# Attention of a hybrid decoder layer on one core: query blocks ascending in every head, K and V loaded in halves of the keys, Q tiles loaded one block further ahead

## The chip, the cores and the metric

The kernel runs on one core of a Trainium2 chip. The metric is the device time of one execution in microseconds (us). The kernel before was run three times: 1775.66, 1776.54 and 1775.54 us, median 1775.66.

## The reference

One decoder layer over 2048 tokens of width 1024. A projection of x gives latents for attention, two mixer inputs u and v, and gates; eight causal attention heads with 64 + 32 (rotary) columns of q and k and 64 of v run beside a spatial gating unit; both are gated, merged, projected and normalised.

```python
h = jnp.einsum('bsd,dn->bsn', x, w_in[l]) + b_in[l]
c_q, c_kv, k_pe, z_a, u, v, z_b, g_a, g_b = split_columns(h)
y_a = mla_attention(c_q, c_kv, k_pe, cos, sin, g_q[l], w_uq[l], g_kv[l], w_ukv[l]) * jax.nn.silu(z_a)
y_b = spatial_gating(u, v, sgu_ln_g[l], sgu_ln_b[l], w_s[l], b_s[l]) * jax.nn.silu(z_b)
merged = (jax.nn.sigmoid(g_a) * jnp.einsum('bsc,cd->bsd', y_a, w_oa[l])
          + jax.nn.sigmoid(g_b) * jnp.einsum('bsc,cd->bsd', y_b, w_ob[l]))
x = layer_norm(DN_ALPHA * x + jnp.einsum('bsd,de->bse', merged, w_out[l]), ln_g[l], ln_b[l])
# inside mla_attention, for every head and block of queries
s = jnp.einsum('bqhd,bkhd->bhqk', q[:, start:end], k[:, :end]).astype(jnp.float32) * scale
p = jax.nn.softmax(jnp.where(causal, s, -jnp.inf), axis=-1)
outs.append(jnp.einsum('bhqk,bkhd->bqhd', p.astype(v.dtype), v[:, :end]))
```

## The kernel before

Every float32 product runs as three passes of float32r operands: each operand is split into a head (hi) and a remainder (lo) by `split` (ACT casts hi, L65; DVE subtracts for lo, L66), and hi·hi + hi·lo + lo·hi is accumulated (`mm`, L86, issues every matmul). There are four phases.

Phase 1 makes q, k and v of all heads as (hi, lo) and stores them to DRAM (`qnd`, `qrd` for q without and with position, `kd`, `krd` for k, `vd`). Phase 2 makes gelu(v) for the spatial gating unit and mixes it within chunks: `mix(c, ...)` multiplies into `psm`, sums into `um` (four additions of `sgb` on DVE, L468), transposes to `ptu`, copies to one of two buffers `mo` (ACT, L474) and stores to `mxd` on GpSimd's (POOL's) queue (L475), four stores a chunk. The last chunk's `mix(*pend)` ends the phase. Before it, the last tile is normalised (`gv`, L450, then split into `vh`, `vl`).

Phase 3 is the attention with the products of the gates in between. `gates()` is a generator of steps of three matmuls, called "filler" here: `weights(m)` loads a block of weights (`fst`, L498) and splits it (`fwh` on ACT, `fwl` on DVE); `group` accumulates eight steps into a bank `psg`, of which there are two; DVE (`fo`, L522) or ACT takes the result out. 48 steps of it run ahead of the attention. The attention is cut into 64 blocks of 256 queries of a head. A block's `score()` makes one tile of scores `pss` (up to 512 keys, four banks), three matmuls `Kh,Q`, `Kl,Q`, `Kh,Q`; after a row's last tile ACT's exponentials (L642, `pr`) free the row's banks. `turn()` transposes two key tiles of probabilities (L658), `product()` multiplies them with V into `po`. TensorE's order in this phase is written by a loop that plans with assumed lags (`LAG_*`) and gives the filler `FILL` = 1.19 of the attention's time; score steps run at most one block ahead of the turns (`si <= ti + 1`). The other engines' orders, SP's DMA queue among them, are left to the scheduler. `ls`, the row sums, is cleared by a MEMSET on DVE (L691) before the loop.

`head(h)` loads a head's K and V whole (`Kh`, `Kl` as two DMAs each, L588/L589; `V`, L590), two buffers each; head 0's K comes in a piece of 512 keys and one of 1536. A `Block` loads its Q tile (L603/L604), two buffers. `block(n)` makes block n, and with the second block of a head loads the next head; `block(si + 1)` is called when a block's scores are all issued. Even heads run their blocks ascending (2 key tiles up to 16), odd heads descending:

```python
order = [(h, qc if h % 2 == 0 else 7 - qc) for h in range(H) for qc in range(8)]
```

Phase 4 gates, merges, projects and normalises.

Of the kernel before, what the change touches and what calls it, by code (L numbers as in the profile page):

```python
# [15 lines left out]
F32 = mybir.dt.float32  # L16
# [3 lines left out]
ALU = mybir.AluOpType  # L20
# [13 lines left out]
W = 512           # width of each mixer  # L34
C = 512           # tokens of a chunk
# [6 lines left out]
# inv_freq[i] = 10000 ** (-2 i / 32) in float32  # L42
# [7 lines left out]
# 128-wide column blocks of the gates  # L50
# [3 lines left out]
FILL = 1.19       # time of the gates' products per time of the attention's  # L54
# [3 lines left out]
def hybrid_layer_kernel(ctx, tc, xT, x, pos, invf, w_lat, b_lat, w_v, b_v,  # L58
# [37 lines left out]
    # by chunk: attention before its normalisation, mixed v, gates  # L96
# [5 lines left out]
    # ----------------------------------------------------------- constants  # L102
# [7 lines left out]
    # keep where q - k >= 0  # L110
# [7 lines left out]
    # x^T, two chunks of tokens on chip, each as (hi, lo)  # L118
# [22 lines left out]
    # ======================================================= 1: q, k and v  # L141
# [10 lines left out]
    # latent weights, with the first chunk of x  # L152
# [20 lines left out]
    # rope tables: cos, sin of pos * inv_freq for all tokens  # L173
# [24 lines left out]
    # cos(r) = sin(pi/2 - |r|)  # L198
# [6 lines left out]
    # up projections, with the rms gains (and the score scale) folded in  # L205
# [21 lines left out]
    def rope(dst, src, t0, n, heads, nm):  # L227
        """dst[P, n*heads, 32] = rope(src); tables of token tiles t0 .. t0+n"""
# [16 lines left out]
    def latent(c, ts):  # L245
        """latents of token tiles ts: bias, rms norm, rope of k"""
# [44 lines left out]
    def up(c, lh, ll):  # L291
        """k, v and q of a chunk, in four parts"""
# [16 lines left out]
        for t in range(4):  # L309
            tk = slice(t * P, (t + 1) * P)  # L310
            # q rope
# [8 lines left out]
            # k nope, head pairs  # L320
# [4 lines left out]
            # v  # L325
# [10 lines left out]
            # q nope, head pairs  # L336
# [24 lines left out]
    # ============================== 2: v of the spatial gating unit, mixed  # L361
    with ExitStack() as ph:
# [12 lines left out]
        def gelu_v(c, t):  # L375
            """gelu(v) of a token tile and its mean and variance"""
# [21 lines left out]
        # the first tiles along with the last part of phase 1  # L398
# [27 lines left out]
            # [s, g, t]: keep t >= s  # L426
# [51 lines left out]
        for c in (2, 3, 0, 1):  # L478
# [11 lines left out]
            pend = (c, vh, vl)  # L490
        mix(*pend)

    def gates():
        """u, z_b, z_a and the merge gates; steps of three matmuls.
        silu and sigmoid by tanh; the halves are folded in further on."""
        def weights(m):
            st = xs.tile([P, KD, P], F32, tag="st", name="fst")
            sp.dma_start(st, w_feat[m])  # L498
            wh = fw.tile([P, KD, P], F32R, tag="fwh", name="fwh")
            wl = fw.tile([P, KD, P], F32R, tag="fwl", name="fwl")  # L500
            for k in range(0, KD, 4):
                split(st[:, k:k + 4, :], wh[:, k:k + 4, :], wl[:, k:k + 4, :])
            return wh, wl

        gu, late = {}, []

        def group(m, c, wh, wl):
            xh, xl = xt[c]
            ps = ps_g.tile([P, C], F32, tag="g", name="psg")
            for k in range(KD):  # L510
                mm3(ps, (wh[:, k, :], wl[:, k, :]), (xh[:, k, :], xl[:, k, :]),
                    k == 0, k == KD - 1)
                if k < KD - 1:
                    yield
            o = fw.tile([P, C], F32, tag="fo", name="fo")
            if m >= MT_GA:
                # 2 sigmoid - 1
                act.activation(o, ps, AF.Tanh, scale=0.5, bias=bfh[:, m:m + 1])
                pool.dma_start(gd[c][m], o)  # L519
                yield  # L520
                return
            dve.tensor_scalar(o, ps, bft[:, m:m + 1], None, op0=ALU.add)  # L522
            late.append(finish(m, c, o))
            next(late[-1])
            yield

        def finish(m, c, o):
            """the activation of a group, its parts between the next steps"""
            t = fw.tile([P, C], F32, tag="ft", name="ft")
            if MT_U <= m < MT_ZB:  # L530
                # 2 gelu(u) = u (1 + tanh(c (u + a u^3)))
                act.activation(t, o, AF.Square)
                yield
                dve.tensor_scalar(t, t, 0.044715, 1.0, op0=ALU.mult, op1=ALU.add)
                dve.tensor_tensor(t, t, o, op=ALU.mult)
                act.activation(t, t, AF.Tanh, scale=float(np.sqrt(2.0 / np.pi)))
                yield
                g = fw.tile([P, C], F32, tag="gu", bufs=3, name="gu")
                dve.scalar_tensor_tensor(g, t, 1.0, o, op0=ALU.add, op1=ALU.mult)
                gu[m - MT_U, c] = g  # L540
            else:
                # 2 silu(z) = z (1 + tanh(z / 2))
                act.activation(t, o, AF.Tanh, scale=0.5)
                yield
                dve.scalar_tensor_tensor(o, t, 1.0, o, op0=ALU.add, op1=ALU.mult)
                if m >= MT_ZB:
                    dve.tensor_tensor(o, o, gu.pop((m - MT_ZB, c)), op=ALU.mult)
                pool.dma_start(gd[c][m], o)

        for cs2 in ((0, 1), (2, 3)):  # L550
            # two blocks at a time where the chunks of x are exchanged
            ms_ = [[m] for m in MT_ORDER]
            ms_ = (ms_[:-2] + [ms_[-2] + ms_[-1]] if cs2[0] == 0 else
                   [ms_[0] + ms_[1]] + ms_[2:])
            for ms in ms_:
                w = {m: weights(m) for m in ms}
                for c in cs2:
# [376 lines left out]
```

## Time and profile before

| What | Value |
|---|---|
| runs, median of 3 | 1775.66 us |
| profiled execution: span from first to last instruction | 1775.5 us |
| mean granted TensorE clock in it | 0.992 |
| TensorE (PE) busy | 98% of the span |
| DVE, ACT, POOL busy | 62%, 43%, 8% |
| DMA, mean over the span | 129 GB/s |

The profiled execution's own time is its span; the page gives no other beside it. PE is TensorE's matmuls, PEld its weight loads, DVE VectorE, ACT ScalarE, POOL GpSimd, SPq the queue of DMAs that SyncE issues. A wait is idle time of an engine just before an instruction, put down to what released it last. The granted clock is a share of TensorE's full clock. Times in the rows are microseconds from the start of the span.

### The profile page before, as it was taken

The page shows a single profiled execution, that of the slowest core. Times are in us where ns is not written, and L with a number is a line of the kernel's source. Part 1 is how long each engine was busy: PE and PEld are TensorE (multiplying, and loading weights), DVE is VectorE, ACT ScalarE, POOL GpSimd, SP SyncE. Part 2 cuts the span into 40 slices and gives each one's busy share as a digit, 9 for nine tenths or more (in the row PEclk, how much of TensorE's full clock was granted, in tenths as well). Part 3 has the DMA queues.
Part 4 walks back from the last instruction along what each step waited for, and adds up shares of the span by engine and source line. Part 5 has one row for each costly group of instructions (what it writes and reads, how often), then busy time and mean ns, then how long its engine had stood idle before and what let it go on. Part 6 is the DMA issues. An engine that isn't in the chain of part 4 may idle for free.

```text
span 1775.5 us, 25048 instructions
## 1 busy us (share of the span) xinstructions
PE 1731.4 (98%) x9249; PEld 1484.1 (84%) x9249; DVE 1094.2 (62%) x2209; ACT 754.6 (43%) x1708; POOL 134.3 (8%) x231
## 2 busy tenths in 40 slices
PE   7999999899999999999999999999999999999998
PEld 7999887788888888888788888888888877888886
DVE  6765686476664555444776666654445478777664
ACT  6533442255544454545655445544544341303020
POOL 0000011100000100000100000100001000000000
PEclk9999999999999999999999999999999999999999
DMA  6564851631321422422713212321123886657341
GB/s 220 194 196 160 276 170 38 181 99 49 101 72 66 140 68 66 119 68 75 215 62 89 76 55 81 122 72 59 60 66 120 283 270 225 215 197 215 120 131 72
DMA packets 111100, 229.06 MB, mean 129 GB/s; under 512 B 13120, under 2 KB 41920, under 8 KB 108608
## 3 DMA queue, kind: packets, MB, share of 16 engines
q1 hardware_dynamic: 99968, 193.88, 34.9%
q0 software_dynamic: 11008, 33.57, 5.4%
q8 instruction: 73, 1.20, 0.3%
q14 instruction: 51, 0.42, 0.1%
HBM read 155.50 MB, written 71.89 MB: 128 GB/s over the span
## 4 chain that ended last, share of the span: by engine, by line
PE 45%; issue 41%; DMA 5%; POOL 4%; DVE 3%; ACT 2%; SPq 0%; POOLq 0%; DVEq 0%; ACTq 0%
PE po L86 11%; PE psg L86 9%; PE psa L86 4%; PE psl L86 4%; PE pb L86 4%; PE pa L86 4%; PE pss L86 3%; PE pt L658 2%; POOL gd L519 2%; DMA wost<-in_w_out_dram 1%; PE psq L86 1%; POOL otd L686 1%; DMA xst<-in_xT_dram 1%; DMA mxd<-mo 1%; PE psr L86 1%
## 5 line engine op out<-in xcount | busy, mean ns | idle before, releaser
L86 PE MATMUL psg<-xh,fwh 128*128 128x512 f32 x896 | 375.3, 419 | 4.9 <-DVE fo L522 4.9
L66 DVE TENSOR_TENSOR pl<-pt,ph 128x512 fp32r<-128x512 f32 (+2 forms) x352 | 199.7, 567 | 287.2 <-ACT ph L65 285.5
L86 PE MATMUL psg<-xl,fwh 128*128 128x512 f32 x896 | 354.5, 396 | 0.0
L86 PE MATMUL psg<-xh,fwl 128*128 128x512 f32 x896 | 354.1, 395 | 0.0
L65 ACT CAST ph<-pt 128x512 fp32r<-128x512 f32 (+2 forms) x352 | 172.0, 489 | 241.4 <-PE pt L658 208.8
L642 ACT ACTIVATE pr<-pss,nm 128x512 f32<-128x512 f32 (+2 forms) x320 | 198.0, 628 | 114.9 <-DVE nm L639 95.9
L86 PE MATMUL pss<-Kh,Q 96*128 96x512 f32 (+3 forms) x640 | 222.5, 377 | 12.9 <-DMA Q<-qrd 7.2
L86 PEld LDWEIGHTS psg<-xh,fwl 128*128 128x128 f32 x896 | 169.6, 189 | 38.4
L636 DVE TENSOR_REDUCE mx<-pss 128x1 f32<-128x384 f32 (+2 forms) x288 | 175.6, 619 | 29.4 <-PE pss L86 26.1
L86 PEld LDWEIGHTS psg<-xh,fwh 128*128 128x128 f32 x896 | 170.6, 190 | 25.6 <-issue 5.3
L86 PEld LDWEIGHTS psg<-xl,fwh 128*128 128x128 f32 x896 | 171.4, 191 | 20.7
L658 PE MATMUL pt<-ident,pr 128*128 128x128 f32 x1088 | 167.2, 274 | 0.0
L86 PEld LDWEIGHTS pss<-Kh,Q 96*128 96x128 f32 x640 | 119.3, 189 | 30.7 <-ACT pr L642 9.7
L658 PEld LDWEIGHTS pt<-ident,pr 128*128 128x128 f32 x1088 | 125.6, 141 | 5.8 <-ACT pr L642 0.4
L86 PEld LDWEIGHTS po<-ph,V 128*128 128x128 f32 x576 | 108.7, 189 | 26.0 <-ACT ph L65 3.2
L86 PE MATMUL pss<-Kl,Q 96*128 96x512 f32 (+2 forms) x320 | 115.9, 362 | 0.0
L86 PE MATMUL po<-pl,V 128*128 128x256 f32 x576 | 113.9, 279 | 0.2
L86 PE MATMUL po<-ph,V 128*128 128x256 f32 x576 | 112.8, 276 | 1.2 <-DVE o L685 0.7
L86 PEld LDWEIGHTS po<-pl,V 128*128 128x128 f32 x576 | 96.5, 190 | 11.3 <-DVE pl L66 1.2
L86 PE MATMUL po<-woh,mh 128*128 128x512 f32 x256 | 100.8, 394 | 1.2 <-ACT mh L65 1.2
L86 PE MATMUL po<-woh,ml 128*128 128x512 f32 x256 | 100.4, 393 | 0.0
L86 PE MATMUL po<-wol,mh 128*128 128x512 f32 x256 | 99.7, 390 | 0.0
(208 smaller groups left out, 2986.3 us busy)
## 6 DMA issues: line engine op xcount, KB each, us to landing
fst<-in_w_feat_dram SPq DMA_DIRECT2D x56, 512.0 KB, 3.7
gd<-fo POOLq DMA_DIRECT2D x96, 256.0 KB, 2.3
wabst<-in_w_ab_dram SPq DMA_DIRECT2D x32, 512.0 KB, 4.2
xst<-in_xT_dram SPq DMA_DIRECT2D x31, 512.0 KB, 4.9
kd<-e SPq DMA_DIRECT2D x16, 512.0 KB, 3.2
vd<-ve SPq DMA_DIRECT2D x16, 512.0 KB, 4.1
qnd<-e SPq DMA_DIRECT2D x16, 512.0 KB, 4.7
Q<-qnd SPq DMA_DIRECT2D x64, 128.0 KB, 2.9
```

The source lines that it names most:

```text
L65: act.copy(hi, src)
L66: dve.tensor_tensor(lo, src, hi.bitcast(F32), op=ALU.subtract)
L86: inorder(pe.matmul(*args, **kw))
L519: pool.dma_start(gd[c][m], o)
L636: dve.tensor_reduce(self.mx[:, i:i + 1], ps[:, :n], axis=AX.X, op=ALU.max)
L642: act.activation(pr[:, k0:k0 + ne], pe_[:, :ne], AF.Exp, bias=self.nm, accum_out=ls[:, self.h, 2 * self.qc + j, e:e + 1])
L658: inorder(pe.transpose(pt[:, i, j * P:(j + 1) * P], self.pr[j][:, (k + i) * P:(k + i + 1) * P], ident))
L686: pool.dma_start(otd[self.qc // 2][self.h * DV:(self.h + 1) * DV, self.qc % 2 * 256:(self.qc % 2 + 1) * 256], o2)
```

## The change

In the attention, all heads run their blocks ascending. `head(h, half)` loads K and V of half of the keys (1024): the first half has two buffers, the second one. A head's second half is loaded with its third block, the next head's first half with its fifth. Q has three buffers and is loaded one block further ahead. No tile of scores goes across key 1024. `gates` stands ahead of phase 2, and its first weights are asked for before the last `mix(*pend)`. Comments are gone. The core of the diff:

```diff
-        mix(*pend)
+        first = gates(fw, ps_g)
+        next(first)
+        mix(*pend)
...
+                if cs2[0] == 0 and ms is ms_[0]:
+                    yield
...
-    fill = gates()
+    fill = first
     for _ in range(48):
         next(fill)
...
-        def head(h):
-            Kh = kp.tile([DH, S], F32R, tag="Kh", name="Kh")
-            Kl = kp.tile([DH, S], F32R, tag="Kl", name="Kl")
-            Vt = kp.tile([P, NT, 2 * DV], F32R, tag="V", name="V")
-            for ks in (slice(0, 512), slice(512, S)) if h == 0 else (slice(0, S),):
-                for i, K in enumerate((Kh, Kl)):
-                    sp.dma_start(K[:DN, ks].bitcast(F32), kd[h // 2, h % 2 * DN:(h % 2 + 1) * DN, i, ks])
-                    sp.dma_start(K[DN:, ks].bitcast(F32), krd[:, i, ks])
-            sp.dma_start(Vt.bitcast(F32), vd[h])
-            return Kh, Kl, Vt
+        def head(h, half):
+            ks = slice(half * S // 2, (half + 1) * S // 2)
+            Kt = [kp.tile([DH, S // 2], F32R, tag=f"K{e}{half}", bufs=2 - half, name=f"K{e}") for e in "hl"]
+            Vt = kp.tile([P, NT // 2, 2 * DV], F32R, tag=f"V{half}", bufs=2 - half, name="V")
+            for sl in (slice(0, 512), slice(512, S // 2)) if h == 0 and half == 0 else (slice(0, S // 2),):
+                dl = slice(half * S // 2 + sl.start, half * S // 2 + sl.stop)
+                for i, K in enumerate(Kt):
+                    sp.dma_start(K[:DN, sl].bitcast(F32), kd[h // 2, h % 2 * DN:(h % 2 + 1) * DN, i, dl])
+                    sp.dma_start(K[DN:, sl].bitcast(F32), krd[:, i, dl])
+            sp.dma_start(Vt.bitcast(F32), vd[h][:, half * NT // 2:(half + 1) * NT // 2, :])
+            return Kt + [Vt]
...
-                self.Qt = kp.tile([DH, 2, 256], F32R, tag="Q", name="Q")
+                self.Qt = kp.tile([DH, 2, 256], F32R, tag="Q", bufs=3, name="Q")
...
-                    nb = 2 * qc + j + 1             # key blocks, in even tiles of at most four
-                    nt = -(-nb // 4)
-                    ends = [-(-nb * (i + 1) // nt) * P for i in range(nt)]
+                    nb = 2 * qc + j + 1
+                    ends = []
+                    for lo, hi in ((0, min(nb, 8)), (8, nb)):
+                        nt = -(-(hi - lo) // 4)
+                        ends += [(lo + -(-(hi - lo) * (i + 1) // nt)) * P for i in range(nt)]
+                    nt = len(ends)
...
-        order = [(h, qc if h % 2 == 0 else 7 - qc) for h in range(H) for qc in range(8)]
+        order = [(h, qc) for h in range(H) for qc in range(8)]
...
-                if n % 8 == 1 and h + 1 < H:
-                    hds[h + 1] = head(h + 1)
+                if n == 0:
+                    hds[0, 0] = head(0, 0)
+                if qc == 2:
+                    hds[h, 1] = head(h, 1)
+                if qc == 4 and h + 1 < H:
+                    hds[h + 1, 0] = head(h + 1, 0)
                 blocks[n] = Block(h, qc, hds)
-        block(0)
-        block(1)
+        for n in range(3):
+            block(n)
...
-                    block(si + 1)
+                    block(si + 2)
```

What it moves is seen on three places. The first is SP's queue between phases 2 and 3, where the burst of loads for the attention begins; before:

```order
L498 DMA fst<-in_w_feat_dram 128x1024 [waits DMAHW6_49,DVE_49]
L603 DMA Q<-qnd 64x2x256 [waits PE_49,DVE_49,Activation_49,Pool_49]
L604 DMA Q<-qrd 32x2x256
L588 DMA Kh<-kd 64x512
L589 DMA Kh<-krd 32x512
L588 DMA Kl<-kd 64x512
L589 DMA Kl<-krd 32x512 [waits DMAHW7_49]
L588 DMA Kh<-kd 64x1536 [waits DMAHW0_49]
```

and in the change:

```order
L366 DMA fst<-in_w_feat_dram 128x1024 [waits DMAHW6_49,DVE_49]
L594 DMA Kh<-kd 64x512 [waits DVE_49,PE_49,Pool_49]
L595 DMA Kh<-krd 32x512
L594 DMA Kl<-kd 64x512
L595 DMA Kl<-krd 32x512
L594 DMA Kh<-kd 64x512
L595 DMA Kh<-krd 32x512 [waits DMAHW7_49]
```

The Q tile that led the burst now comes behind the first half of K and V of head 0. Its waits before end with the last addition into `um` on DVE (L468, of the last `mix`); those of K's first load in the change end, on DVE, with the last split of `vl` (L66), which comes ahead of that `mix`. The second place is SP's queue at the start of a head, before at head 2:

```order
L498 DMA fst<-in_w_feat_dram 128x1024 [waits DMAHW5_49,DVE_49]
L588 DMA Kh<-kd 64x2048 [waits PE_49]
L589 DMA Kh<-krd 32x2048
L588 DMA Kl<-kd 64x2048 [waits DMAHW0_49]
L589 DMA Kl<-krd 32x2048 [waits DMAHW1_49]
L603 DMA Q<-qnd 64x2x256 [waits DMAHW2_49]
L604 DMA Q<-qrd 32x2x256 [waits DMAHW3_49]
```

where the Q tile behind the burst is that of the head's second block; and in the change, where the first four K loads are the first half of the head that follows, the other four the second half of this head, and the Q tile behind them is that of its third block:

```order
L366 DMA fst<-in_w_feat_dram 128x1024 [waits DMAHW7_49,DVE_49,Activation_49]
L594 DMA Kl<-kd 64x1024 [waits DMAHW0_49,PE_49]
L594 DMA Kh<-kd 64x1024 [waits DMAHW1_49,PE_49]
L595 DMA Kh<-krd 32x1024 [waits DMAHW2_49]
L595 DMA Kl<-krd 32x1024 [waits DMAHW3_49]
L594 DMA Kl<-kd 64x1024 [waits DMAHW4_49,PE_49]
L594 DMA Kh<-kd 64x1024 [waits DMAHW5_49,PE_49]
L595 DMA Kh<-krd 32x1024 [waits DMAHW6_49]
L595 DMA Kl<-krd 32x1024 [waits DMAHW7_49]
L609 DMA Q<-qnd 64x2x256 [waits DMAHW0_49]
L610 DMA Q<-qrd 32x2x256 [waits DMAHW1_49]
```

The loads are twice as many and half as large, and both bursts hold 1.5 MB of K. The third place is TensorE at the first row of nine key blocks, in the fifth block of head 0; before:

```order
L86 MATMUL psg<-xh_2940,fwl 128x512
L86 MATMUL pss<-Kh,Q 128x384
L86 MATMUL pss<-Kl,Q 128x384
L86 MATMUL pss<-Kh,Q 128x384
L86 MATMUL psg<-xh_2940,fwh 128x512
```

and in the change:

```order
L86 MATMUL psg<-xh_2940,fwl 128x512
L86 MATMUL pss<-Kh,Q 128x512
L86 MATMUL pss<-Kl,Q 128x512
L86 MATMUL pss<-Kh,Q 128x512
L86 MATMUL psg<-xh_2940,fwh 128x512
```

The row's first tile is 512 keys wide where it was 384; its last is 128. Up to this place TensorE's order is the same in both.

## Rows read from the trace of the kernel before

**Rows 1.** The page: busy time (share) and instructions of PE.

```profile
PE 1731.4 (98%) x9249; PEld 1484.1 (84%) x9249; DVE 1094.2 (62%) x2209; ACT 754.6 (43%) x1708; POOL 134.3 (8%) x231
```

**Rows 2.** Waits of PE: engine, line, releaser: us in total, times, longest.

```profile
PE pss L86 <- DMA Q<-qrd: 7.2, 3, 3.1
...
PE pss L86 <- ACT pr L642: 5.4, 6, 2.2
```

**Rows 3.** Timeline, phase 2 to 3: start, us, engine, operation, [idle before <- releaser].

```profile
310.74 0.69 DVE L66 TENSOR_TENSOR vl<-gv,vh 128x512 fp32r<-128x512 f32 x1 [0.68 <-ACT vh L65]
...
318.55 0.59 SPq L603 DMA_DIRECT2D Q<-qnd  x1
...
319.89 1.30 POOL L475 DMA_DIRECT2D mxd<-mo  x2 [7.86 <-ACT mo L474]
...
324.67 0.59 ACT L474 COPY mo<-ptu 128x512 f32<-128x512 f32 x1 [2.21 <-DMA mxd<-mo]
...
337.94 0.48 DVE L691 MEMSET ls<- 128x512 f32 x1 [8.47 <-DMA mxd<-mo]
...
339.77 0.76 PE L86 MATMUL psg<-xh,fwh 128*128 128x512 f32 x1 [4.87 <-DVE fo L522]
```

**Rows 4.** Stretches: engines busy, granted clock, DMA share, GB/s.

```profile
320.00:340.00 20.00, 15.13 (x70) 12.28 (x69) 6.57 (x11) 4.90 (x10) 2.27 (x4) 0.98 0.98 268
340.00:360.00 20.00, 19.96 (x81) 16.22 (x82) 11.55 (x22) 8.42 (x19) 2.16 (x4) 0.85 0.48 152
600.00:620.00 20.00, 16.87 (x95) 14.85 (x93) 9.46 (x28) 7.81 (x24) 2.17 (x4) 0.91 0.73 197
860.00:880.00 20.00, 18.80 (x103) 16.12 (x104) 17.04 (x41) 15.78 (x42) 2.34 (x5) 1.00 0.83 279
1020.00:1040.00 20.00, 17.79 (x89) 14.99 (x87) 11.79 (x24) 8.36 (x21) 1.11 (x2) 0.91 0.15 47
1100.00:1140.00 40.00, 37.10 (x208) 32.45 (x207) 26.44 (x65) 20.49 (x57) 4.33 (x8) 0.96 0.49 145
```

**Rows 5.** DMAs issued from 326.5 to 326.95: KB each, us to landing.

```profile
mxd<-mo POOLq DMA_DIRECT2D x1, 256.0 KB, 10.8
```

**Rows 6.** Timeline at the start of head 2, SP and PE.

```profile
599.54 0.46 SPq L588 DMA_DIRECT2D Kh<-kd  x1
...
602.37 0.60 SPq L604 DMA_DIRECT2D Q<-qrd  x1
...
611.56 0.41 PE L86 MATMUL pss<-Kh,Q 96*128 96x384 f32 x1 [3.13 <-DMA Q<-qrd]
```

**Rows 7.** Timeline of PE at 1026.87; waits of PE from 860 to 985.

```profile
1026.87 0.50 PE L86 MATMUL pss<-Kh,Q 96*128 96x512 f32 x1 [2.21 <-ACT pr L642]
...
PE pss L86 <- DMA Q<-qrd: 1.4, 1, 1.4
PE pss L86 <- ACT pr L642: 0.9, 2, 0.5
```

**Rows 8.** Timeline of PE: score matmuls in a row, four widths.

```profile
598.28 0.28 PE L86 MATMUL pss<-Kl,Q 96*128 96x128 f32 x1
598.39 0.44 PE L86 MATMUL pss<-Kh,Q 96*128 96x128 f32 x2
598.67 0.28 PE L86 MATMUL pss<-Kl,Q 96*128 96x256 f32 x1
598.79 0.28 PE L86 MATMUL pss<-Kh,Q 96*128 96x256 f32 x1
...
1021.14 0.34 PE L86 MATMUL pss<-Kl,Q 96*128 96x384 f32 x1
1021.31 0.34 PE L86 MATMUL pss<-Kh,Q 96*128 96x384 f32 x1
...
1021.96 0.39 PE L86 MATMUL pss<-Kl,Q 96*128 96x512 f32 x1
1022.19 0.39 PE L86 MATMUL pss<-Kh,Q 96*128 96x512 f32 x1
```

More of the change, by code (lines that the diff above doesn't have):

```diff
@@ L359, in hybrid_layer_kernel, with gates, weights, group @@
     lctx.close()
+    def gates(fw, ps_g):
+        def weights(m):
+            st = xs.tile([P, KD, P], F32, tag="st", name="fst")
+            sp.dma_start(st, w_feat[m])
+            wh = fw.tile([P, KD, P], F32R, tag="fwh", name="fwh")
+            wl = fw.tile([P, KD, P], F32R, tag="fwl", name="fwl")
+            for k in range(0, KD, 4):
+                split(st[:, k:k + 4, :], wh[:, k:k + 4, :], wl[:, k:k + 4, :])
+            return wh, wl
+        gu, late = {}, []
+        def group(m, c, wh, wl):
+            xh, xl = xt[c]
+            ps = ps_g.tile([P, C], F32, tag="g", name="psg")
+            for k in range(KD):
+                mm3(ps, (wh[:, k, :], wl[:, k, :]), (xh[:, k, :], xl[:, k, :]),
+                    k == 0, k == KD - 1)
+                if k < KD - 1:
+                    yield
+            o = fw.tile([P, C], F32, tag="fo", name="fo")
+            if m >= MT_GA:
+                act.activation(o, ps, AF.Tanh, scale=0.5, bias=bfh[:, m:m + 1])
+                pool.dma_start(gd[c][m], o)
+                yield
+                return
+            dve.tensor_scalar(o, ps, bft[:, m:m + 1], None, op0=ALU.add)
+            late.append(finish(m, c, o))
+            next(late[-1])
+            yield
+        def finish(m, c, o):
+            t = fw.tile([P, C], F32, tag="ft", name="ft")
+            if MT_U <= m < MT_ZB:
+                act.activation(t, o, AF.Square)
+                yield
+                dve.tensor_scalar(t, t, 0.044715, 1.0, op0=ALU.mult, op1=ALU.add)
+                dve.tensor_tensor(t, t, o, op=ALU.mult)
+                act.activation(t, t, AF.Tanh, scale=float(np.sqrt(2.0 / np.pi)))
+                yield
+                g = fw.tile([P, C], F32, tag="gu", bufs=3, name="gu")
+                dve.scalar_tensor_tensor(g, t, 1.0, o, op0=ALU.add, op1=ALU.mult)
+                gu[m - MT_U, c] = g
+            else:
+                act.activation(t, o, AF.Tanh, scale=0.5)
+                yield
+                dve.scalar_tensor_tensor(o, t, 1.0, o, op0=ALU.add, op1=ALU.mult)
+                if m >= MT_ZB:
+                    dve.tensor_tensor(o, o, gu.pop((m - MT_ZB, c)), op=ALU.mult)
+                pool.dma_start(gd[c][m], o)
+        for cs2 in ((0, 1), (2, 3)):
+            ms_ = [[m] for m in MT_ORDER]
+            ms_ = (ms_[:-2] + [ms_[-2] + ms_[-1]] if cs2[0] == 0 else
+                   [ms_[0] + ms_[1]] + ms_[2:])
+            for ms in ms_:
+                w = {m: weights(m) for m in ms}
+                if cs2[0] == 0 and ms is ms_[0]:
+                    yield
+                for c in cs2:
+                    pieces = (x_pieces(2) if c == 1 and ms is ms_[-1] else
+                              x_pieces(3) if c == 2 and ms is ms_[0] else iter(()))
+                    for m in ms:
+                        for n, _ in enumerate(group(m, c, *w[m])):
+                            if n % 2 == 0:
+                                next(pieces, None)
+                            yield
+                            late[:] = [f for f in late if next(f, f) is not f]
+                    for _ in pieces:
+                        pass
@@ L490, in hybrid_layer_kernel @@
             pend = (c, vh, vl)
+        first = gates(fw, ps_g)
+        next(first)
         mix(*pend)
[L493 to L557, printed above, removed]
-                    pieces = (x_pieces(2) if c == 1 and ms is ms_[-1] else
-                              x_pieces(3) if c == 2 and ms is ms_[0] else iter(()))
-                    for m in ms:
-                        for n, _ in enumerate(group(m, c, *w[m])):
-                            if n % 2 == 0:
-                                next(pieces, None)
-                            yield
-                            late[:] = [f for f in late if next(f, f) is not f]
-                    for _ in pieces:
-                        pass
@@ L604, in __init__ @@
                 sp.dma_start(self.Qt[DN:].bitcast(F32), qrd[h // 4, h % 4 * DR:(h % 4 + 1) * DR, :, qs])
-                if h not in hds:
-                    hds[h] = head(h)
-                self.Kh, self.Kl, self.Vt = hds[h]
+                self.kv2 = hds
                 self.todo = []
@@ L625, in score @@
                 ps = ps_s.tile([P, 512], F32, tag="s", name="pss")
-                ks = slice(k0, k0 + n)
-                mm(ps[:, :n], Qh, self.Kh[:, ks], start=True, stop=False)
-                mm(ps[:, :n], Qh, self.Kl[:, ks], start=False, stop=False)
-                mm(ps[:, :n], Ql, self.Kh[:, ks], start=False, stop=True)
+                Kh, Kl, _ = self.kv2[self.h, k0 * 2 // S]
+                ks = slice(k0 % (S // 2), k0 % (S // 2) + n)
+                mm(ps[:, :n], Qh, Kh[:, ks], start=True, stop=False)
+                mm(ps[:, :n], Qh, Kl[:, ks], start=False, stop=False)
+                mm(ps[:, :n], Ql, Kh[:, ks], start=False, stop=True)
                 if last:
```

2 lines of the change are left out of this document (1 added, 1 removed).

## The prediction

> **What bounds the kernel now.** I began with the page's busy shares: TensorE is busy for 1731.4 of 1775.5 us, 98% [rows 1]. So the time falls only with idle time of TensorE, with stretches at a lower clock, or with less matmul work. The median of the runs, 1775.66 us, stands 0.16 above this profiled span; the sum is made on 1775.5 and 0.16 is added at its end. A measurement here tells 0.2%, 3.6 us, from no change.
>
> Next come TensorE's waits. Inside the attention two kinds matter: 7.2 us in three waits of score matmuls for a Q tile, and 5.4 us in six waits of score matmuls for ACT's exponentials, which free the score banks [rows 2]. The timeline between phases 2 and 3 holds a third kind, one wait of 4.87 us [rows 3]. The windows add what a wait costs afterwards. The mean granted clock is 0.98 and 0.85 in the two stretches of 20 us from 320, 0.91 from 600, 0.91 from 1020 and 0.96 over the 40 us from 1100; but it is 1.00 from 860 [rows 4], where the shortest of the three Q waits, 1.4, lies [rows 7]. Read as time lost, that is (0.02 + 0.15)x20 = 3.4, then 0.09x20 = 1.8, again 1.8, and 0.04x40 = 1.6 us.
>
> **Phase 2 to 3: the wait of 4.87 us.** Read the timeline backwards [rows 3]. TensorE's gate product at 339.77 waits for DVE's `fo`, which frees a gate bank. DVE was held by the MEMSET of `ls`, which starts at 337.94 after 8.47 us idle: `ls` takes over space of phase 2, so it waits for all stores of mixed v (`mxd`). The last store, issued near 326.9, lands 10.8 us later [rows 5]. It meets a burst that SP begins at 318.55: in the old order a Q tile leads it, and waits for DVE's last sums of the mixing. The burst moves two heads' K and V and three Q tiles, 3 + 2 + 0.6 = 5.6 MB (1.5 MB of K and 1 MB of V a head, 0.19 a Q).
>
> In the new order K leads the burst, and of DVE it waits only for the split `vl`, which ends at 310.74 + 0.69 = 311.43 [rows 3]. The burst begins 7 us sooner, and moves one and a half heads and three Q tiles, 3.75 + 0.56 = 4.3 MB. At 0.59 us an issue [rows 3] the first eight small K pieces, 0.75 MB, are out by 316; from there I take 268 GB/s, the rate of the first stretch with the old burst [rows 4]. By 326.9 some 0.75 + 10.9x0.268 = 3.7 MB are moved of 4.3 and the four stores' 1.0; the other 1.6 take 6 us, so the last store lands near 333 instead of 337.7. TensorE would have been ready at 339.77 - 4.87 = 334.9, and gets its product 1.83 us after the MEMSET's start, so a MEMSET by 333.1 costs nothing. I leave 1.3 us over for stores that land a little later than this estimate. The Q wait of 1.4 had no lower clock behind it, so one of 1.3 should have none either and the 3.4 go too: 4.9 + 3.4 - 1.3 = **-7.0**; bounds -8.3 and 0.
>
> **The Q waits.** All three are at the start of an even head, after an odd one that ended on its smallest block. At the first, the K burst for a coming head starts at 599.54, the second piece of the Q tile is issued behind it at 602.37, and TensorE waits for it until 611.56, for 3.13 us [rows 6]: 12.0 us from the burst's start to a usable tile. The new order has the same 1.5 MB in the burst, now halves of two heads, but the Q behind it belongs to the head's third block, not its second; and the head before ends on its block of 16 key tiles. Between the last scores of that block, which release the burst, and the scores of the third block lie its turns, 8x4 transposes, and its products, 32, each some 0.11 us like a short matmul [rows 8], with gate products at 1.19 of that time in between: 64x0.11x2.19 = 15.4 us, besides two small blocks. That is over 12.0. The old junctions where a head ends on its large block (0 to 1, 2 to 3, 4 to 5, 6 to 7) bear this out: the three waits are all at the others. So 7.2 of waiting and the clock behind it, 1.8 at 600 and 1.6 at 1100, go: **-10.6**; bounds -10.6 and 0. The 40 more DMAs that SP issues, 24 us in all, lie on a queue that TensorE waits for at these three places only, so I cost them at nothing; without the cover of a block's lead each would cost its 0.6 us at the burst it stands in, four at a head, 2.4 us.
>
> **The banks.** Blocks 2 to 5 of an ascending head put nine to twelve score matmuls in a row, where four banks are all there is until ACT frees one. The old odd heads, descending, hold such rows too, with wider tiles, and the longest of the six waits, 2.21 at 1026.87, is in one; the ascending head from 860 to 985 waits 0.9 in two [rows 7]. The old price is 5.4 + 1.8 of clock = 7.2. With every head ascending I give the seven after the first the price of that head, 7x0.9 = 6.3: **-0.9**; bounds -7.2 (no wait) and 7x2.21 - 7.2 = +8.3.
>
> **The score tiles.** A row of scores no longer has a tile across key 1024. Nine key blocks turn from 384+384+384 columns into 512+512+128, ten from 512+384+384 into 512+512+256, thirteen from 512+3x384 into 2x512+384+256; other rows, and the number of matmuls, stay. Start to start a matmul takes 0.23 us at 512 columns, 0.17 at 384, 0.12 at 256 and 0.11 at 128 [rows 8]. Three passes of nine blocks: 3x(0.57 - 0.51) = 0.18; of ten and of thirteen 3x(0.35 - 0.34) = 0.03 each. Eight heads: **+1.9**; bounds 0 and that.
>
> **First filler weights sooner.** The call stands earlier in the program, but up to the attention the instructions of TensorE, ACT, DVE and POOL come in the same order as before, and SP's up to the burst: **0**, both bounds too.
>
> Sum: -7.0 - 10.6 - 0.9 + 1.9 = -16.6, so 1758.9, and with the 0.16 **1759.1 us**.
>
> **The rivals.** *A: the stores stay late.* The four stores pass through two buffers of `mo`, so the third copy waits for the first store: 2.21 us on ACT before 324.67 [rows 3]. That store was issued at 319.89, just as the old burst began; in the new order it meets a burst 8 us old. If it takes the last one's 10.8 us, the third store is issued only near 331, the last lands near 337 or later, and the wait with its clock stays: 7.0 back, 1766.1. For it: 10.8 us for a store inside the burst [rows 5]. Against: the first store landed 4.8 us after its issue, with K of the same burst already issued around it. By the Trainium skill ("DMA: Bandwidth & Descriptors", section "Queues, rings and completion order") each DMA engine takes turns, packet by packet, between the queue rows that have work, so that it would matter whether a burst runs and not how much of it is queued: that gives A. By that rule the rows of 10.8 and 4.8 should be alike; they are not, which is why A stays the smaller case.
>
> *B: the banks cost twice as much*, 1.8 us at each of seven heads, because a head's first blocks now always follow a block of 16 key tiles, with ACT still at its exponentials: 12.6 - 7.2 = +5.4 in place of -0.9, 1765.4.
>
> *C, slower than before: the banks and the clock.* If every head has a wait like that at 1026.87, 2.21 with 1.8 of lower clock behind it, the banks cost 7x4.0 = 28 us, 20.8 more than before: 1759.1 + 0.9 + 20.8 = 1780.8. It decides from (15.7 + 7.2)/7 = 3.3 us a head on. For it: the waits of over 2 us had a lower clock behind them [rows 2, 4]. Against: of the three old ascending heads with a head before them none waited 2 us for a bank.
>
> *D: the change does not do what it says.* The stores stay late as in A, and the Q waits return as waits for those halves of K and V that have one buffer instead of two, whose loads start only when the head before is done with them: 1775.66 + 1.9 - 0.9 = 1776.7. Against it: those halves are first read at the head's fifth block.
>
> **How the numbers follow.** Forecast 0.46; A 0.24, B 0.17, C 0.05, D 0.08. Faster by over 0.2% means below 1772.1: the forecast, A and B, 0.87. D gives no change, 0.08; C slower, 0.05. The range: all bounds down (phase 2 to 3 -8.3, Q -10.6, banks -7.2, tiles 0) give 1749.6, so 1750 below; above, A with half of B's extra, 1769. C, D and the whole of A with B are left out.
>
> **What would show it.** Right: no wait of a score matmul for Q; the MEMSET of `ls` by 334 and the gate product after it at most 1.3 us late; SP's burst from 311 or 312; clock near 1.00 from 340 to 360 and from 600 to 620; score matmuls waiting 5 to 8 us in all for ACT's `pr`. A is shown by a MEMSET idle until 337 or later and stores of 10 us from the first on; B by over 10 us of waits for `pr`; C by those waits and a clock of 0.91 once a head; D by waits for K, V or Q. The prediction is wrong if the three Q waits are still there, or if a new releaser of TensorE costs more than 5 us.

## The result, and the profile after

The change took 1760.02 us, the median of four runs (1758.64 to 1761.87), against 1775.6 us: a ratio of 0.9914, interval 0.9900 to 0.9928. That is faster, 15.6 us where 16.5 were forecast, and inside the range. The profiled execution has a span of 1759.5 us and a time of its own of 1761.38; so this run's time lies 1.9 us above its span. The spans differ by 1775.5 - 1759.5 = 16.0.

The total agrees better than its parts. The page's busy share, and TensorE's waits from 300 us on:

```profile
PE 1728.6 (98%) x9249; PEld 1476.2 (84%) x9249; DVE 1090.0 (62%) x2209; ACT 752.5 (43%) x1708; POOL 134.3 (8%) x231
```

```profile
PE psg L86 <- DVE fo L390: 3.7, 1, 3.7
PE pb L86 <- ACT wabh L65: 2.3, 1, 2.3
PE pss L86 <- ACT pr L650: 2.1, 2, 1.1
```

Against [rows 2] the three Q waits are gone, and of 5.4 us in six waits for ACT's exponentials 2.1 in two are left. The wait between phases 2 and 3 is still there. The windows, the same stretches as [rows 4]:

```profile
320.00:340.00 20.00, 16.27 (x67) 13.08 (x66) 7.94 (x14) 5.67 (x10) 1.41 (x3) 0.91 0.79 226
340.00:360.00 20.00, 20.00 (x93) 16.59 (x92) 11.53 (x25) 7.48 (x17) 2.16 (x4) 0.92 0.41 124
600.00:620.00 20.00, 20.00 (x118) 17.59 (x116) 10.47 (x27) 10.10 (x27) 2.17 (x4) 1.00 0.29 98
1020.00:1040.00 20.00, 20.00 (x111) 17.06 (x109) 13.81 (x26) 9.49 (x22) 1.68 (x3) 1.00 0.21 66
1100.00:1140.00 40.00, 40.00 (x228) 34.80 (x227) 26.09 (x63) 22.78 (x63) 4.38 (x8) 1.00 0.29 93
```

In the windows from 600 on the clock is 1.00 where it was 0.91 to 0.96, and TensorE is busy all the time. Between phases 2 and 3 it is 0.91 and 0.92: (0.09 + 0.08)x20 = 3.4 us lost, as before. The timeline of that place, to be laid beside [rows 3]:

```profile
310.66 0.51 SPq L594 DMA_DIRECT2D Kh<-kd  x1
...
319.03 1.30 POOL L554 DMA_DIRECT2D mxd<-mo  x2 [7.86 <-ACT mo L553]
...
325.86 0.59 ACT L553 COPY mo<-ptu 128x512 f32<-128x512 f32 x1 [4.25 <-DMA mxd<-mo]
...
335.95 0.48 DVE L699 MEMSET ls<- 128x512 f32 x1 [5.21 <-DMA mxd<-mo]
...
337.78 0.76 PE L86 MATMUL psg<-xh,fwh 128*128 128x512 f32 x1 [3.73 <-DVE fo L390]
```

SP's burst starts 7.9 us sooner. The first store takes 325.86 - 319.03 = 6.8 us instead of 4.8, so the copies and stores behind it come later (325.86 instead of 324.67); the last store, issued at 328.12 and not near 326.9, lands sooner after its issue than the 10.8 us of [rows 5]. From the DMAs issued from 328.1 to 328.2 (KB each, us to landing):

```profile
mxd<-mo POOLq DMA_DIRECT2D x1, 256.0 KB, 7.6
```

Both nearly cancel: the MEMSET starts at 335.95 instead of 337.94, and the wait is 3.73 instead of 4.87.

Where the 16.0 us came from can be cut at three marks, the first score, the first product of phase 4, and the end. Before, the first score matmul of the attention is at 353.6 and the first `pb` at 1411.76; after they are at

```profile
351.25 0.22 PE L86 MATMUL pss<-Kh,Q 96*128 96x128 f32 x1
...
1394.59 0.39 PE L86 MATMUL pb<-ybh,wabh 128*128 128x512 f32 x1
```

Up to the first score 2.3 us are gained (1.1 of it the shorter wait; the rest mostly lies in phase 1, which the change doesn't touch), over the attention 1058.2 - 1043.3 = 14.8, and phase 4 gives back 1.2, with 2.3 us of wait for its weights `wabh` where it had 2.1. The first and the last of these three are no more than two executions of one kernel differ by: a second profile of the kernel before (below) has its first score at 351.28, 1057.8 us of attention and 364.7 us behind it, where the change has 364.9. So the attention carries the gain. Its windows from the first score to the first `pb`, before, after, and with the order of the blocks alone (below), give its length and TensorE's busy time in it:

```profile
353.58:1411.76 1058.18, 1043.81 (x5747) 904.60 (x5745) 612.32 (x1237) 535.64 (x1307) 85.22 (x156) 1.00 0.30 94
351.25:1394.59 1043.34, 1040.60 (x5747) 897.39 (x5746) 607.43 (x1236) 533.40 (x1307) 85.23 (x156) 1.00 0.31 95
346.89:1390.33 1043.44, 1038.92 (x5747) 899.72 (x5746) 610.11 (x1237) 535.67 (x1307) 85.75 (x157) 1.00 0.31 95
```

TensorE is idle for 14.4 us in the first, 2.7 in the second and 4.5 in the third.

### The profile page after: what moved, and what is told of

Its sections match the earlier page's. It is cut to its first block, busy times and chain, and to the rows that moved or that the text cites. A ratio compares the mean times of both kernels' runs of the same rounds, so it can differ in the third digit from the quotient of the medians.

```text
span 1759.5 us, 25118 instructions
## 1 busy us (share of the span) xinstructions
PE 1728.6 (98%) x9249; PEld 1476.2 (84%) x9249; DVE 1090.0 (62%) x2209; ACT 752.5 (43%) x1708; POOL 134.3 (8%) x231
## 4 chain that ended last, share of the span: by engine, by line
PE 70%; issue 17%; DVE 4%; DMA 4%; ACT 2%; POOL 2%; POOLq 0%; DVEq 0%; SPq 0%; ACTq 0%
PE psg L86 23%; PE po L86 15%; PE pss L86 8%; PE pt L666 5%; PE pb L86 4%; PE pa L86 4%; PE psa L86 4%; PE psl L86 4%; PE psq L86 1%; DMA xst<-in_xT_dram 1%; POOL gd L387 1%; DMA wost<-in_w_out_dram 1%; DMA mxd<-mo 1%; PE psr L86 1%; POOL otd L694 1%
## 5 line engine op out<-in xcount | busy, mean ns | idle before, releaser
L66 DVE TENSOR_TENSOR pl<-pt,ph 128x512 fp32r<-128x512 f32 (+2 forms) x352 | 199.7, 567 | 315.0 <-ACT ph L65 313.3
L644 DVE TENSOR_REDUCE mx<-pss 128x1 f32<-128x512 f32 (+3 forms) x288 | 176.1, 619 | 11.8 <-PE pss L86 9.0
L65 ACT CAST wabh<-wabst 128x1024 fp32r<-128x1024 f32 x32 | 33.7, 1052 | 158.2 <-PE pa L86 134.8
```

Of the source, the lines that this page charges most:

```text
L65: act.copy(hi, src)
L66: dve.tensor_tensor(lo, src, hi.bitcast(F32), op=ALU.subtract)
L644: dve.tensor_reduce(self.mx[:, i:i + 1], ps[:, :n], axis=AX.X, op=ALU.max)
```

## The experiments

Two theories for the attention stood open: that the order of the blocks took the Q waits away, or that the third Q tile did. Four kernels bear on it. Each ratio is against runs of the kernel before that were made beside it; their medians are 1773.80, 1775.19 and 1775.33 us, and single runs go from 1770.46 to 1781.62.

**The change with two Q buffers.**

```diff
-                self.Qt = kp.tile([DH, 2, 256], F32R, tag="Q", bufs=3, name="Q")
+                self.Qt = kp.tile([DH, 2, 256], F32R, tag="Q", name="Q")
...
-        for n in range(3):
+        for n in range(2):
             block(n)
...
-                    block(si + 2)
+                    block(si + 1)
```

> The change with two Q buffers, loaded one block ahead as before; order, halves and tiles as in the change. If the order of the blocks is what took the Q waits away (a head now starts behind the turns of a block of 16 key tiles), the three Q waits stay away, at most 1 us in all, and the time stays at 1760 us, 3 either way. If it is the third buffer, all seven head starts wait 1.4 to 3.1 us for Q, as the three did, 10 to 22 us in all and more with the clock: 1772 us or over.

Measured: 1758.96 us (1758.77 to 1760.81), ratio 0.9914 (0.9894 to 0.9935), no wait for Q, and 1043.3 us from the first score to the first `pb`, as in the change. The third buffer does nothing here. Of the rows of its waits from 300 us on:

```profile
PE psg L86 <- DVE fo L390: 3.2, 1, 3.2
...
PE pss L86 <- ACT pr L650: 2.1, 2, 1.1
```

**The order alone.**

```diff
-        order = [(h, qc if h % 2 == 0 else 7 - qc) for h in range(H) for qc in range(8)]
+        order = [(h, qc) for h in range(H) for qc in range(8)]
```

> The kernel before with every head ascending, nothing else: K and V whole, two Q buffers, old score tiles. If the order takes the Q waits away: no Q wait, waits for ACT's exponentials near the 2 us of the change instead of 5.4, the wait of 4.9 us between phases 2 and 3 as before: 1775.6 - 7.2 - 3.4 (clock) - 3 - 1.8 (clock) = 1760 us, 3 either way. If the third buffer takes them away: Q waits at seven head starts instead of three, 1780 us or more.

Measured: 1760.15 us (1756.53 to 1762.41), ratio 0.9917 (0.9893 to 0.9941), and 1043.4 us from the first score to the first `pb`, where the change has 1043.3: this one line is as fast as the whole change. Its waits:

```profile
PE pss L86 <- ACT pr L642: 3.2, 5, 0.8
...
PE psg L86 <- DVE fo L522: 2.1, 1, 2.1
```

The Q waits are gone with K and V whole and two Q buffers, and the long waits for the exponentials (the longest 2.2 before) are gone with them: the longest is 0.8. The wait for `fo` is a surprise: up to the burst and through it this kernel's instructions come in the order of the kernel before, and yet it waits 2.1 us and not 4.9. Its first store landed sooner: the third copy was held for 0.86 us,

```profile
322.26 0.59 ACT L474 COPY mo<-ptu 128x512 f32<-128x512 f32 x1 [0.86 <-DMA mxd<-mo]
```

against 2.21 in [rows 3], and in the 20 us from 320 the DMA engines moved 284 GB/s where they moved 268 [rows 4]. So this wait differs by some 3 us between profiles whose instructions up to here are the same. Whether that is chance or something in the kernel, one profile of each cannot tell; this one is of the fastest of its four runs.

The rows of SP and PE at the start of head 2 show what the order does for the Q tile of the second block:

```profile
574.19 0.41 SPq L589 DMA_DIRECT2D Kl<-krd  x1
574.64 0.54 SPq L603 DMA_DIRECT2D Q<-qnd  x1
...
602.07 0.42 PE L86 MATMUL pss<-Kh,Q 96*128 96x384 f32 x1
```

The tile still stands right behind the burst of K, but its scores come 27 us later; before, TensorE was ready for them some 7 us after the tile's issue (601.79 to 608.43).

**Three Q tiles under the old order.** The first of two tries (the third block is also made ahead of the loop, and `o1` has one buffer to make room):

```diff
-                self.Qt = kp.tile([DH, 2, 256], F32R, tag="Q", name="Q")
+                self.Qt = kp.tile([DH, 2, 256], F32R, tag="Q", bufs=3, name="Q")
...
-                if n % 8 == 1 and h + 1 < H:
+                if n % 8 == 2 and h + 1 < H:
...
-                    block(si + 1)
+                    block(si + 2)
```

> The kernel before with three Q tiles loaded one block further ahead and the next head's K and V asked for with a head's third block, so that the Q tile behind the burst is the third block's; heads alternate as before (and one buffer for o1, to make room). If a block's lead alone is enough, the three Q waits shrink from 7.2 to under 1 us and the clock behind them stays: 1775.6 - 10 = 1765 us, with the waits for ACT's exponentials at 5 us as before. If it is the order that matters, the Q waits stay over 4 us and the time over 1770 us.

Measured: 1784.72 us (1782.58 to 1785.59), ratio 1.0055, slower, with Q waits of 11.5 us in two and a new one of 3.9 for gate weights. Neither theory had that. The timeline of SP at the start of head 2 gives the reason:

```profile
595.68 0.59 SPq L589 DMA_DIRECT2D Kl<-krd  x1
605.96 0.34 SPq L590 DMA_DIRECT2D V<-vd  x1
606.35 0.54 SPq L603 DMA_DIRECT2D Q<-qnd  x1
606.94 0.60 SPq L604 DMA_DIRECT2D Q<-qrd  x1
```

The scheduler put V's load ahead of the Q tiles. V waits for the last product of the head before, SP issues in order, and so the Q tiles stood behind that wait until 606 and came at 611.95, after 5.67 us of wait. The run doesn't test the lead, since the lead was lost to the queue.

**The lead alone, second try.** The same, with K of the next head asked for with a head's fourth block and V, in a function of its own, with its sixth (the diff is against the first try):

```diff
-                if n % 8 == 2 and h + 1 < H:
-                    hds[h + 1] = head(h + 1)
+                if n % 8 == 3 and h + 1 < H:
+                    hds[h + 1] = head(h + 1)
+                if n % 8 == 5 and h + 1 < H:
+                    vts[h + 1] = head_v(h + 1)
```

> The kernel before with heads alternating as before, but three Q tiles loaded one block further ahead, the next head's K asked for with a head's fourth block and its V with its sixth, so that neither K's nor V's wait stands ahead of the Q tiles of the first blocks. If a Q tile's place behind the burst makes the Q waits: none over 0.5 us, the clock of 0.91 behind two of them gone, waits for ACT's exponentials still near 5 us: 10 us under the kernel before, 1765 us. If the waits come from the descending order itself (the next block's scores follow too soon for any load), they stay over 4 us and the time is within 4 us of the kernel before.

Measured: 1767.15 us (1764.0 to 1768.98), ratio 0.9950 (0.9934 to 0.9967). Its waits:

```profile
PE psg L86 <- ACT fwh L65: 6.0, 1, 6.0
PE pss L86 <- ACT pr L646: 5.4, 6, 2.2
PE psg L86 <- DVE fo L522: 2.0, 1, 2.0
```

No Q wait; 5.4 us for the exponentials, in six as before; and a new wait of 6.0 for gate weights (TensorE resumes at 867.48), whose load SP issues at 862.18, right behind a Q tile at 861.47; what made it late was not tried. From the first score to the first `pb` it takes 1052.8 us. At head 2 a Q tile now goes out just ahead of the burst:

```profile
593.58 0.60 SPq L607 DMA_DIRECT2D Q<-qrd  x1
594.23 0.59 SPq L587 DMA_DIRECT2D Kh<-kd  x1
```

So a Q tile behind the burst makes the Q waits where its scores follow soon. This kernel takes the tile from behind the burst; the order leaves it there and puts the scores off. Either removes the waits. The third buffer, the earlier request of Q and the later one of K and V came together here, and none of them was run by itself. What the order does besides, and the lead doesn't, is to shorten the waits for the exponentials: 5.4 here and in the kernel before, 2.1 and 3.2 with ascending heads.

**The score tiles alone**, `ends` as in the change, in the kernel before:

```diff
-                    nt = -(-nb // 4)
-                    ends = [-(-nb * (i + 1) // nt) * P for i in range(nt)]
+                    ends = []
+                    for lo, hi in ((0, min(nb, 8)), (8, nb)):
+                        nt = -(-(hi - lo) // 4)
+                        ends += [(lo + -(-(hi - lo) * (i + 1) // nt)) * P for i in range(nt)]
+                    nt = len(ends)
```

> The kernel before with the score tiles cut at key 1024 as in the change, nothing else. By the durations of single matmuls 1.9 us more of TensorE, less what was idle anyway: 1775 to 1778 us, the Q waits and the waits for ACT's exponentials as before (7 and 5 us). If the narrow last tiles free the banks sooner, the waits for the exponentials fall from 5.4 towards the 2.1 of the change and the time is the same or lower.

Measured: 1774.93 us against 1775.33, ratio 0.9998 (0.9987 to 1.0009), no difference. Q waits 7.0 us, waits for the exponentials 4.3 in five:

```profile
PE pss L86 <- DMA Q<-qrd: 7.0, 3, 2.7
...
PE pss L86 <- ACT pr L645: 4.3, 5, 1.6
```

First score to first `pb` is 1056.9 us against 1058.2. The waits for the exponentials are about 1 us shorter; the whole run's interval, 2 us to either side, cannot tell what the tiles cost in columns.

**The weights at their old place.** In the change, `first = gates(...)` and its first step behind the last `mix`:

```diff
-        first = gates(fw, ps_g)
-        next(first)
         mix(*pend)
...
-    fill = first
+    fill = gates(fw, ps_g)
+    next(fill)
```

> The change with the first gate weights asked for after the last mixing, as before. The order of the instructions is the same on every engine, so every theory expects the time of the change, 1760 us, 3 either way, and the same waits; it shows how far two sets of runs of one order differ.

Measured: 1758.02 us (1757.12 to 1762.44), ratio 0.9908 (0.9891 to 0.9926), the time of the change; 1043.6 us from the first score to the first `pb`, and a wait of 3.0 for `fo`.

The other four kernels are about the wait between phases 2 and 3, where the prediction missed. First **the kernel before once more**, profiled:

> The kernel before, profiled beside the kernels of this call. Every theory expects the three Q waits (7 us), the waits for ACT's exponentials (5 us) and one wait between phases 2 and 3. Open is how far that last one, 4.87 us in the profile shown, moves from execution to execution: if it is set by how many bytes of the burst are queued, it stays within 1 us; if by how the queues share the DMA engines, it may be anything from 2 to 6 us.

Measured: 1775.49 us, span 1773.8. Its waits for Q, the exponentials and `fo`:

```profile
PE pss L86 <- DMA Q<-qrd: 7.0, 3, 2.9
PE pss L86 <- ACT pr L642: 5.4, 6, 2.2
PE psg L86 <- DVE fo L522: 4.6, 1, 4.6
```

The first two repeat to 0.2 us. The third is 4.6 here and 4.7 with the tiles alone, within the 1 us that goes with the bytes queued; but it is 2.1 with the order alone, whose burst is the same, and 1.8 and 2.0 in the two tries with three Q tiles, and that goes with the queues' sharing. Which of the two sets it stays open.

**The row sums apart**, in the change:

```diff
+        lsp = ph.enter_context(tc.tile_pool(name="p3l", bufs=1))
+        ls = lsp.tile([P, H, NT, 4], F32, name="ls")
         kp = ph.enter_context(tc.tile_pool(name="p3k", bufs=2))
...
-        ls = sm.tile([P, H, NT, 4], F32, tag="ls", bufs=1, name="ls")
         dve.memset(ls, 0.0)
```

> The change with the row sums in a pool of their own ahead of K, so that their MEMSET no longer takes over the space of the mixing's stores; DVE then does not wait for the stores. If the stores are the whole of the wait between phases 2 and 3: the wait of 3.7 us and the clock behind it (3.4 us) go, 1753 us, 2 either way. If the gate weights or SP's burst are late next: a new wait of 1 to 4 us in the same place and 1756 to 1760 us.

Measured: 1756.07 us (1754.43 to 1756.99), ratio 0.9893 (0.9868 to 0.9917). The MEMSET runs at 310.99 and the wait for `fo` is gone from the list. `pb` in phase 4 waits 5.4 us for its weights instead of 2.3, and phase 4 is 2.0 us longer than in the change: some of the gain goes there. But the edit did a second thing. SP's burst waits for the last addition into `um` again, as in the kernel before, and starts 7.3 us later than in the change:

```profile
317.94 0.51 SPq L596 DMA_DIRECT2D Kh<-kd  x1
```

So this run does not tell the MEMSET's place from the start of the burst; the next one, whose burst starts when it did before, does.

**Order and row sums**, the order of the change and the row sums apart in the kernel before, and nothing else of the change:

> The kernel before with two edits alone: every head ascending, and the row sums in a pool of their own whose MEMSET waits for no store; K and V whole, two Q buffers, old score tiles. If the order and the MEMSET are all that counts: no Q wait, no wait between phases 2 and 3, 1753 to 1757 us, at or under the change with the same pool (1756.1). If halves, tiles or the third Q buffer carry some of the gain: 1759 us or more.

Measured: 1756.40 us (1754.42 to 1757.46), ratio 0.9891 (0.9858 to 0.9924). One Q wait of 0.3 us is in its list, and no wait for DVE's `fo`. The last store of that kernel, in the DMAs issued from 326.5 to 326.6, lands at 335.3, about as late as in the change, and TensorE doesn't wait for it, since DVE has made the MEMSET at 311.34:

```profile
mxd<-mo POOLq DMA_DIRECT2D x1, 256.0 KB, 8.8
```

```profile
311.34 0.48 DVE L692 MEMSET ls<- 128x512 f32 x1 [0.17 <-DVE vl L66]
```

So it is the MEMSET's place in memory that makes the wait, not the lateness of the stores by itself.

**Three places for `mo`**, in the change:

```diff
-                mo = wk.tile([P, C], F32, tag="mo", name="mo")
+                mo = wk.tile([P, C], F32, tag="mo", bufs=3, name="mo")
```

> The change with three buffers for mo instead of two: the third copy no longer waits for the first store, so the third and fourth stores can be issued some 5 and 1 us sooner. If rival A's chain (copy behind a late store) holds the MEMSET, the wait between phases 2 and 3 falls from 3.7 us to under 2 and the time by 2 us, by 5 with the clock: 1755 to 1758 us. If the last store lands only when the burst is through, whenever it was issued, the wait stays over 3 us and the time at 1760.

Measured: 1762.91 us (1755.3 to 1764.16), ratio 0.9920 (0.9893 to 0.9948), wait 3.6. It doesn't decide: the third copy is free, but the fourth now waits for the first store, 3.94 us until 326.54, and is only 0.7 us sooner than with two buffers (327.24).

```profile
326.54 0.59 ACT L553 COPY mo<-ptu 128x512 f32<-128x512 f32 x1 [3.94 <-DMA mxd<-mo]
```

**Four places**, the fourth being a buffer of the finished `gv`:

```diff
-                mo = wk.tile([P, C], F32, tag="mo", bufs=3, name="mo")
+                mo = va.tile([P, C], F32, tag="gv", bufs=4, name="mo") if m == 3 and c == 1 else wk.tile([P, C], F32, tag="mo", bufs=3, name="mo")
```

> The change with four places for the copies of the last mixing (three of mo, one of the finished gv), so that none of the last four copies waits for a store and all four stores are issued by about 323 us. If it is the chain copy behind store that sets the MEMSET: the stores have landed by 331, the MEMSET starts within 1 us of the work ahead of it on DVE, the wait of 3.7 us and the clock behind it go: 1753 to 1757 us, as with the row sums apart (1756.1). If a store lands only with the end of the burst, whenever it is issued: landing near 335 again, a wait over 3 us, 1760 us.

Measured: 1755.52 us (1754.94 to 1756.7), ratio 0.9889 (0.9874 to 0.9904), no wait for `fo`. The four stores are issued by 323.2:

```profile
321.16 1.29 POOL L554 DMA_DIRECT2D mxd<-mo  x2 [9.70 <-ACT mo L553]
322.65 1.07 POOL L554 DMA_DIRECT2D mxd<-mo  x2 [0.20 <-issue]
```

But the run did a second thing that was not meant: with the larger pool SP's burst waits for the stores, and starts only behind them.

```profile
327.55 0.51 SPq L594 DMA_DIRECT2D Kh<-kd  x1
```

The stores then had the DMA engines without the burst, so the run does not show what the copies alone would give. What it does show is that a burst 17 us later than that of the change makes TensorE wait for no load: the first score is at

```profile
346.61 0.22 PE L86 MATMUL pss<-Kh,Q 96*128 96x128 f32 x1
```

against 351.25 in the change. The three versions without the wait, at 1755.5, 1756.1 and 1756.4, lie 3.6 to 4.5 us under the change and differ by less than their intervals. Their twelve runs, 1754.4 to 1757.5, are all under the four of the change (1758.6 to 1761.9), but the intervals of the ratios overlap with its, and single runs of other kernels that have the wait come down to 1755.3. The version of two edits is the smallest.

## Why the prediction was right, and where it was not

Of the signs it named, the three Q waits are gone, the burst starts at 310.66 and the clock is 1.00 from 600 to 620. The MEMSET came at 335.95 and not by 334, the gate product behind it 3.73 us late and not 1.3, the clock from 340 to 360 is 0.92, and the waits for `pr` are 2.1 us and not 5 to 8. No wait for K or V is in the list, so D fell.

- **The Q waits, -10.6.** Right: 7.2 us of waiting and the lower clock from 600 and from 1100 are gone. The mechanism was right with too small a margin. After the change, at the start of head 2 (timeline of SP and PE), the second four K loads of the burst start at 577.12 (the first four at 569.74), the Q tile's second piece goes out at 579.93, and the third block's first score is at 610.10:

```profile
577.12 0.45 SPq L594 DMA_DIRECT2D Kl<-kd  x1
...
579.93 0.60 SPq L610 DMA_DIRECT2D Q<-qrd  x1
...
610.10 0.42 PE L86 MATMUL pss<-Kh,Q 96*128 96x384 f32 x1
```

  That is 33 us against my 15.4. The gate products were priced too low: I gave them 1.19 of 64x0.11, 8.4 us, but 87 of them lie between 577.1 and 606.7, some 20 us at the 0.23 of [rows 8] (an estimate). With so much, the second block's tile is in time too: with two buffers its second piece goes out at 576.42 and its scores are at 604.88. The prediction credited the third buffer and the order together; the order alone does it.

- **Phase 2 to 3, -7.0.** Wrong: -1.1 of waiting and nothing of the clock in the profiled run. The step that failed is "the last store lands near 333". Its rate was right (271 GB/s from 316 to 326.9, where it took 268), but it took the stores' issue times from the old trace. In the change the first store takes 2.0 us longer beside the early burst, the copies behind it come 1.2 later, and the last store is issued at 328.12 and not at 326.9. That is 1.2 of the 2.7 us by which it missed 333; for the rest, the store took 7.6 us where the sum left it 6, and why is open. It lands at 335.7. That is the chain of rival A, which came half true, at a price of 5.9 us against the sum instead of 7.0. And the term was sized on one execution of a wait that reads 4.9, 4.6 and 4.7 in three profiles and 2.1 with the order alone, with nothing changed at this place in any of them (3.0, 3.2 and 3.7 in three profiles with the early burst), so even the sign of 1.1 us is not shown. The old burst held two Q tiles, not three (they go out at 318.55 and 330.81, the next at 355.17); no term rests on that.

  The reading of the queues stays open too: the first and the last store take 6.8 and 7.6 us in the change, and took 4.8 and 10.8 before. By the Trainium skill ("DMA: Bandwidth & Descriptors", section "Queues, rings and completion order"), cited with rival A, each DMA engine takes turns, packet by packet, between the queue rows that have work. That rule would have the two alike: the change agrees with it, and the rows of before are not what it alone gives.

- **The banks, -0.9.** Mis-sized, in the other direction: 5.4 + 1.8 of clock became 2.1 with none, -5.1, and 0.8 us of waits of `po` went as well (1.2 before in three, 0.4 after in one). I priced seven heads at the 0.9 of one old ascending head, but the other old ascending heads show none, and 4.5 of the old 5.4 lie in descending ones. In the change the 2.1 lie in two of the eight heads. The runs with the old order keep 4.3 to 6.3 and those with the new one have 2.1 to 3.3. Rivals B and C fall with that.

- **The score tiles, +1.9.** About right in size, and given back. Over the attention TensorE is busy 1.7 us longer in the change than with the order alone (1040.6 and 1038.9) and idle 1.8 us less. The second profile with the new order and the old tiles, that with the row sums apart, is busy 1039.7 us, and the six with the new tiles 1040.4 to 1040.9, so the price lies between 0.7 and 2.0. The attention's 14.8 is then 11.6 us less of idle time, 11.3 of it the waits for Q, banks and `po`, and 3.2 less of busy time: 4.9 less with the order alone, which is about the 5.2 at which the clock was priced, and 1.7 more with the rest. **First filler weights, 0:** right. **40 more DMAs, 0:** no cost is seen; the attention takes 1043.3 us in the change with them and 1043.4 with the order alone, without them, though the tiles differ as well.

- **The 0.16 at the end.** The sum was made against 1775.5 as if that execution had the median's time. In every run on record that gives both, a run's time lies 1.65 to 1.88 us over its span (1761.38 to 1759.5, 1775.49 to 1773.8); so the profiled execution of before was probably a run of about 1777.2, slower than the median by 1.6. The difference of spans, 16.0, is the better thing to hold against the -16.6.

So the total came out right by luck: two misses of about 5 us had opposite signs, phase 2 to 3 with 5.9 too little and the attention, where -9.6 was forecast, with 5.2 more. The Q waits alone, the largest term, were right in cause and size.

The runs of the change lie in two groups, spans 1756.8 at a mean clock of 0.998 and 1759.5 to 1760.0 at 0.994 to 0.996. Those of 1756.8 have no profile, but the executions with a wait of 3.0 and 3.2 us at this place (the weights at their old place; two Q buffers) have spans of 1756.3 and 1757.1 and a mean clock of 0.998, and those with 3.6 and 3.7 spans of 1762.3 and 1759.5 and 0.996. That the two groups are this is likely, not shown.

## What to carry to other kernels

When a load is late behind a burst in an in-order queue, look first at what the consumer does just before it: putting the blocks in an order that ends a stage on its longest block gave the load 33 us, and a third buffer then bought nothing. An earlier burst can move other transfers: beside it the first store took 6.8 us instead of 4.8, and the stores behind it were issued later. What waited for them was a MEMSET that had only inherited their memory, and giving it other memory removed the wait with the stores as late as before. Before a change with several parts is kept, each part should be run alone: here one line of the diff carried the gain.

## What was not expected of the hardware

A wait that came with memory taken over from earlier work: a 0.48 us MEMSET held DVE idle for 8.47 us, TensorE for 4.87, and the lower clock behind it (0.98 and 0.85 in the two stretches from 320) took 3.4 more. And the order within one DMA queue: V's load, waiting for a product, kept the Q tiles behind it for 10 us in SP's queue (595.68 to 605.96) and the kernel with more buffers became the slower one, 1784.7 us.
